# FiLM layer on one core: slab 0 loaded by two DMAs and stored in five parts, the other slabs stored whole

## The chip, the cores and the metric

The kernel runs on one core of a Trainium2 chip. The metric is the device time of one execution in microseconds (us). Four runs of the kernel before the change took 84.0, 84.25, 84.34 and 84.47 us; their median is 84.29 us.

## What is computed

The reference scales and shifts every row of `x` by a gamma and a beta that belong to its batch entry:

```
batch, seq, dim, cond_dim = 32, 512, 256, 64      # all float32
gamma = conditioning @ gamma_proj                 # [32, 256]
beta  = conditioning @ beta_proj                  # [32, 256]
out   = x * (1 + gamma[:, None, :]) + beta[:, None, :]
```

`x` and `out` hold 16.78 MB each. All other inputs together hold 0.14 MB.

## The kernel before

`x` is cut into four slabs of eight batch entries (`SLABS`). A slab is one tile `xs0` to `xs3` of 128 partitions by 32 rows by 256 elements (4 MB). Each partition holds 32 rows that follow each other in HBM, so a partition's share of a slab is one run of 32 KB. Sixteen partitions belong to one batch entry, so each partition needs one gamma row and one beta row for the whole slab. All four slabs stay in on-chip memory and are changed in place; no buffer is used twice.

**Loads.** The SyncE queue (SP in the profile) issues all loads of `x` in L60. `LOADS` cuts slab 0 into four DMAs of 8 rows, that is 128 runs of 8 KB each. Slabs 1, 2 and 3 come in one DMA each, 128 runs of 32 KB. The ScalarE queue (ACTq) issues the three small loads, `conditioning` (L49), `gamma_proj` (L51) and `beta_proj` (L52).

**Gamma and beta.** TensorE spreads the transposed conditioning over 512 columns (L73), VectorE copies it out of PSUM (L75), and one matmul for each slab (L80) gives a PSUM tile `gb_p` with the gamma row and the beta row of every partition. ScalarE copies it into `gb_s`, adding 1 to gamma (L83, L86), because GpSimd (POOL) reads `gb_s`, while VectorE (DVE) reads `gb_p`.

**Arithmetic.** Each slab is worked in two groups of 16 rows (`GROUP`). VectorE takes the first 11 rows of a group (`ON_DVE`) with two instructions, L101 (add 1, multiply) and L104 (add beta). GpSimd takes the other 5 rows with L103 (multiply) and L105 (add). In the built program GpSimd does both multiplies of a slab before both adds.

**Stores.** The ScalarE queue issues the stores in L111, behind its own copies. `STORES` gives the rows at which a slab's stores end. Slabs 0 and 3 are stored as two halves of 16 rows (runs of 16 KB), each when its group is done. Slabs 1 and 2 are stored whole (runs of 32 KB) after their second group.

**Semaphores of the DMAs.** The framework gives DMAs completion semaphores from a set of eight and reuses them. A DMA that gets a used one waits on its issuing queue until the earlier DMA of that semaphore has landed. In the kernel before, the load of slab 2 waits in this way for the first load of slab 0, and the load of slab 3 for `beta_proj`.

Of the kernel before, what the change touches and what calls it, by code (L numbers as in the profile page):

```python
# [2 lines left out]

# [5 lines left out]


@with_exitstack
def kernel(
    ctx: ExitStack,
    tc: tile.TileContext,
    x: bass.AP,
    conditioning: bass.AP,
    gamma_proj: bass.AP,
    beta_proj: bass.AP,
    out: bass.AP,  # L20
):
    nc = tc.nc
    f32 = mybir.dt.float32
    ALU = mybir.AluOpType

    batch, seq, dim = x.shape
    cond_dim = conditioning.shape[1]
    P = 128
    SLABS = 4
    BS = batch // SLABS  # L30
    REP = P // BS
    ROWS = BS * seq // P
    assert SLABS * BS == batch and REP * BS == P and ROWS * REP == seq

    x_v = x.flatten_outer_dims().rearrange("(s p r) d -> s p r d", s=SLABS, p=P)
    o_v = out.flatten_outer_dims().rearrange("(s p r) d -> s p r d", s=SLABS, p=P)

    LOADS = {0: [8, 8, 8, 8]}
    STORES = {0: (16, 32), 1: (32,), 2: (32,), 3: (16, 32)}
    GROUP = 16  # L40
    ON_DVE = 11

    consts = ctx.enter_context(tc.tile_pool(name="consts", bufs=1))
    xpool = ctx.enter_context(tc.tile_pool(name="xpool", bufs=1))
    psum = ctx.enter_context(tc.tile_pool(name="psum", bufs=1, space=bass.MemoryType.PSUM))


    cond_s = consts.tile([batch, cond_dim], f32)
    nc.scalar.dma_start(out=cond_s, in_=conditioning)  # L49
    gbproj = consts.tile([cond_dim, 2 * dim], f32)  # L50
    nc.scalar.dma_start(out=gbproj[:, :dim], in_=gamma_proj)  # L51
    nc.scalar.dma_start(out=gbproj[:, dim:], in_=beta_proj)  # L52

    slabs = []
    for s in range(SLABS):
        xs = xpool.tile([P, ROWS, dim], f32, name=f"xs{s}")
        slabs.append(xs)
        r = 0
        for n in LOADS.get(s, [ROWS]):
            nc.sync.dma_start(out=xs[:, r : r + n, :], in_=x_v[s, :, r : r + n, :])  # L60
            r += n
        assert r == ROWS


    ident = consts.tile([batch, batch], f32)
    make_identity(nc, ident)
    rident = consts.tile([batch, batch * REP], f32)
    nc.vector.tensor_copy(  # L68
        out=rident.rearrange("p (b g) -> p b g", g=REP),
        in_=ident.to_broadcast([batch, batch, REP]),  # L70
    )
    cond_T_p = psum.tile([cond_dim, batch * REP], f32)
    nc.tensor.matmul(cond_T_p, lhsT=cond_s, rhs=rident, start=True, stop=True)  # L73
    cond_T = consts.tile([cond_dim, batch * REP], f32)
    nc.vector.tensor_copy(out=cond_T, in_=cond_T_p)  # L75

    gb_p, gb_s = [], []
    for s in range(SLABS):
        p_t = psum.tile([P, 2 * dim], f32, name=f"gb_p{s}")
        nc.tensor.matmul(p_t, lhsT=cond_T[:, s * P : (s + 1) * P], rhs=gbproj,  # L80
                         start=True, stop=True)
        s_t = consts.tile([P, 2 * dim], f32, name=f"gb_s{s}")
        nc.scalar.activation(out=s_t[:, :dim], in_=p_t[:, :dim],  # L83
                             func=mybir.ActivationFunctionType.Identity,
                             bias=1.0, scale=1.0)
        nc.scalar.copy(out=s_t[:, dim:], in_=p_t[:, dim:])  # L86
        gb_p.append(p_t)
        gb_s.append(s_t)

    def rows(t, n):  # L90
        return bass.AP(tensor=t.tensor, offset=t.offset, ap=[t.ap[0], [0, n], t.ap[1]])

    for s in range(SLABS):
        xs = slabs[s]
        g_p, b_p = gb_p[s][:, :dim], gb_p[s][:, dim:]
        g_s, b_s = gb_s[s][:, :dim], gb_s[s][:, dim:]
        for r0 in range(0, ROWS, GROUP):
            v = xs[:, r0 : r0 + ON_DVE, :]
            w = xs[:, r0 + ON_DVE : r0 + GROUP, :]
            nv, nw = ON_DVE, GROUP - ON_DVE  # L100
            nc.vector.scalar_tensor_tensor(out=v, in0=rows(g_p, nv), scalar=1.0, in1=v,  # L101
                                           op0=ALU.add, op1=ALU.mult)
            nc.gpsimd.tensor_tensor(out=w, in0=w, in1=rows(g_s, nw), op=ALU.mult)  # L103
            nc.vector.tensor_add(out=v, in0=v, in1=rows(b_p, nv))  # L104
            nc.gpsimd.tensor_tensor(out=w, in0=w, in1=rows(b_s, nw), op=ALU.add)  # L105
            done = r0 + GROUP
            if done in STORES[s]:
                e0 = 0
                for e1 in STORES[s]:
                    if r0 < e1 <= done or STORES[s] == (ROWS,):  # L110
                        nc.scalar.dma_start(out=o_v[s, :, e0:e1, :], in_=xs[:, e0:e1, :])  # L111
                    e0 = e1


# [1 line left out]
_INS = ['x', 'conditioning', 'gamma_proj', 'beta_proj']  # L116
_OUTS = [((32, 512, 256), 'float32')]


# [23 lines left out]
```

## Time and profile before

| | |
|---|---|
| median of 4 runs | 84.29 us (84.0 to 84.47) |
| the profiled execution | 84.94 us, of which its span is 83.2 us |
| DVE busy | 50.1 us in 18 instructions |
| POOL busy | 46.3 us in 22 instructions |
| PE, ACT busy | 9.1 us, 3.9 us |
| moved by DMA | 33.69 MB, 405 GB/s over the span |

The profiled execution has 1.74 us around its span, and it is 0.65 us above the median of the runs. Times inside the profile count from the start of the span. q1 is the DMA queue of the SyncE engine (the loads of `x`), q10 that of the ScalarE engine (the small loads and all stores). A core has 16 DMA engines, and both queues run on all of them. A DMA over 128 partitions gives each engine 8 packets, one for each contiguous run, and ends with a completion packet of 4 bytes. Besides the views, the trace holds one record for every DMA packet, with queue, size, start and duration, and the time at which each of a DMA's sixteen engines reported completion. Where a text speaks of packet records or completion records, it means these.

### The profile page before, as it was taken

The page shows a single profiled execution, that of the slowest core. Times are in us where ns is not written, and L with a number is a line of the kernel's source. Part 1 is how long each engine was busy: PE and PEld are TensorE (multiplying, and loading weights), DVE is VectorE, ACT ScalarE, POOL GpSimd, SP SyncE. Part 2 cuts the span into 40 slices and gives each one's busy share as a digit, 9 for nine tenths or more (in the row PEclk, how much of TensorE's full clock was granted, in tenths as well). Part 3 has the DMA queues.
Part 4 walks back from the last instruction along what each step waited for, and adds up shares of the span by engine and source line. Part 5 has one row for each costly group of instructions (what it writes and reads, how often), then busy time and mean ns, then how long its engine had stood idle before and what let it go on. Part 6 is the DMA issues. An engine that isn't in the chain of part 4 may idle for free.

```text
span 83.2 us, 155 instructions
## 1 busy us (share of the span) xinstructions
PE 9.1 (11%) x10; PEld 2.8 (3%) x10; DVE 50.1 (60%) x18; ACT 3.9 (5%) x9; POOL 46.3 (56%) x22
## 2 busy tenths in 40 slices
PE   0080499900000000000000000000000000000000
PEld 0010243100000000000000000000000000000000
DVE  1003019999999999965999994399999500000000
ACT  0600033330000000000000000000000000000000
POOL 2000029999999999805999990399999100000000
DMA  2899999969979999997999999699899969899980
GB/s 51 319 435 379 428 422 540 473 299 504 489 339 426 402 536 441 378 457 307 433 449 465 520 394 465 292 504 489 378 394 504 473 299 489 370 441 441 394 378 8
DMA packets 2080, 33.69 MB, mean 405 GB/s; under 512 B 288, under 2 KB 416, under 8 KB 416
## 3 DMA queue, kind: packets, MB, share of 16 engines
q1 hardware_dynamic: 1008, 16.78, 48.1%
q10 hardware_dynamic: 1072, 16.92, 47.5%
HBM read 16.92 MB, written 16.78 MB: 405 GB/s over the span
## 4 chain that ended last, share of the span: by engine, by line
DMA 62%; DVE 15%; ACTq 1%; issue 0%; DVEq 0%
DMA xs<-in_x_dram 53%; DMA gbproj<-in_beta_proj_dram 9%; DVE xs L104 7%; DVE xs L101 7%; ACTq L51 1%; ACTq L49 0%; DVEq L101 0%
## 5 line engine op out<-in xcount | busy, mean ns | idle before, releaser
L103 POOL TENSOR_TENSOR xs<-xs,gb_s 128x1280 f32<-128x1280 f32 x8 | 23.0, 2894 | 17.9 <-ACT gb_s L83 10.9
L101 DVE SCALAR_TENSOR_TENSOR xs<-gb_p,xs 128x2816 f32<-128x2816 f32 x8 | 24.7, 3087 | 9.4 <-ACT gb_s L86 5.1
L104 DVE TENSOR_TENSOR xs<-xs,gb_p 128x2816 f32<-128x2816 f32 x8 | 24.7, 3087 | 0.3
L105 POOL TENSOR_TENSOR xs<-xs,gb_s 128x1280 f32<-128x1280 f32 x8 | 23.0, 2888 | 0.0
L80 PE MATMUL gb_p<-gbproj,cond_T 64*128 64x512 f32 x8 | 7.2, 1074 | 3.1 <-DMA gbproj<-in_beta_proj_dram 3.1
L75 DVE COPY cond_T<-cond_T_p 64x512 f32<-64x512 f32 x1 | 0.7, 683 | 4.8 <-PE cond_T_p L73 4.8
L80 PEld LDWEIGHTS gb_p<-gbproj,cond_T 64*128 64x128 f32 x8 | 2.5, 327 | 7.9 <-issue 7.9
L73 PE MATMUL cond_T_p<-rident,cond_s 32*64 32x512 f32 x2 | 1.9, 1068 | 4.4 <-DMA cond_s<-in_conditioning_dram 4.4
L83 ACT ACTIVATE gb_s<-gb_p 128x256 f32<-128x256 f32 x4 | 1.5, 384 | 11.1 <-PE gb_p L80 11.1
L86 ACT COPY gb_s<-gb_p 128x256 f32<-128x256 f32 x4 | 1.5, 367 | 0.0
L83 ACT ACT_TABLE_LOAD x1 | 1.3, 1283 | 2.4 <-issue 2.4
L68 DVE COPY rident<-ident 32x512 f32<-32x512 f32 x1 | 0.4, 414 | 1.2 <-POOL ident masks.py:199 1.2
L73 PEld LDWEIGHTS cond_T_p<-rident,cond_s 32*64 32x64 f32 x2 | 0.3, 198 | 4.4 <-issue 4.4
masks.py:197 POOL MEMSET ident<- 32x32 f32 x1 | 0.1, 114 | 0.3 <-POOLq L127 0.3
masks.py:199 POOL TENSOR_SCALAR_AFFINE_SELECT ident<-ident 32x32 f32<-32x32 f32 x1 | 0.2, 203 | 0.1
L127 POOL MEMSET const-float32-0.0<- 128x1 f32 x1 | 0.1, 103 | 0.2 <-issue 0.2
L127 POOL MEMSET const-bfloat16-1.0<- 128x1 bf16 x1 | 0.1, 106 | 0.0
L127 POOL MEMSET const-uint8-127<- 128x1 uint8 x1 | 0.1, 106 | 0.0
L127 POOL MEMSET const-float32-1.0<- 128x1 f32 x1 | 0.1, 103 | 0.0
## 6 DMA issues: line engine op xcount, KB each, us to landing
xs<-in_x_dram SPq DMA_DIRECT2D x3, 4096.0 KB, 32.5
out_dram<-xs ACTq DMA_DIRECT2D x4, 2048.0 KB, 17.6
out_dram<-xs ACTq DMA_DIRECT2D x2, 4096.0 KB, 23.9
xs<-in_x_dram SPq DMA_DIRECT2D x4, 1024.0 KB, 8.8
gbproj<-in_gamma_proj_dram ACTq DMA_DIRECT2D x1, 64.0 KB, 6.6
gbproj<-in_beta_proj_dram ACTq DMA_DIRECT2D x1, 64.0 KB, 7.6
cond_s<-in_conditioning_dram ACTq DMA_DIRECT2D x1, 8.0 KB, 3.5
```

Source lines behind the costliest of these rows:

```text
L51: nc.scalar.dma_start(out=gbproj[:, :dim], in_=gamma_proj)
L68: nc.vector.tensor_copy(out=rident.rearrange("p (b g) -> p b g", g=REP), in_=ident.to_broadcast([batch, batch, REP]),)
L73: nc.tensor.matmul(cond_T_p, lhsT=cond_s, rhs=rident, start=True, stop=True)
L75: nc.vector.tensor_copy(out=cond_T, in_=cond_T_p)
L80: nc.tensor.matmul(p_t, lhsT=cond_T[:, s * P : (s + 1) * P], rhs=gbproj, start=True, stop=True)
L83: nc.scalar.activation(out=s_t[:, :dim], in_=p_t[:, :dim], func=mybir.ActivationFunctionType.Identity, bias=1.0, scale=1.0)
L86: nc.scalar.copy(out=s_t[:, dim:], in_=p_t[:, dim:])
L101: nc.vector.scalar_tensor_tensor(out=v, in0=rows(g_p, nv), scalar=1.0, in1=v, op0=ALU.add, op1=ALU.mult)
L103: nc.gpsimd.tensor_tensor(out=w, in0=w, in1=rows(g_s, nw), op=ALU.mult)
L104: nc.vector.tensor_add(out=v, in0=v, in1=rows(b_p, nv))
L105: nc.gpsimd.tensor_tensor(out=w, in0=w, in1=rows(b_s, nw), op=ALU.add)
L127: nc = _bacc.Bacc("TRN2", target_bir_lowering=False, num_devices=1)
```

## The change

Slab 0 is loaded by two DMAs, one of 8 rows and one of 24 rows; the second is described as three runs of 8 KB for each partition (`max_dma_last_dim`). Slab 0 is stored by five DMAs of 2, 2, 4, 8 and 16 rows; the first four are issued after the first group's instructions, the last after the second group's. Slab 3 is stored whole, like slabs 1 and 2. There were 3 small loads, 7 loads of `x` and 6 stores; there are 3, 5 and 8.

```diff
-    LOADS = {0: [8, 8, 8, 8]}
-    STORES = {0: (16, 32), 1: (32,), 2: (32,), 3: (16, 32)}
+    LOADS = {0: [8, 24]}
+    RUN = {0: 8}
+    STORES = {0: (2, 4, 8, 16, 32), 1: (32,), 2: (32,), 3: (32,)}
...
-            nc.sync.dma_start(out=xs[:, r : r + n, :], in_=x_v[s, :, r : r + n, :])
+            nc.sync.dma_start(out=xs[:, r : r + n, :], in_=x_v[s, :, r : r + n, :],
+                              max_dma_last_dim=RUN.get(s, ROWS) * dim * 4)
...
-            done = r0 + GROUP
-            if done in STORES[s]:
-                e0 = 0
-                for e1 in STORES[s]:
-                    if r0 < e1 <= done or STORES[s] == (ROWS,):
-                        nc.scalar.dma_start(out=o_v[s, :, e0:e1, :], in_=xs[:, e0:e1, :])
-                    e0 = e1
+
+            for e0, e1 in zip((0,) + STORES[s], STORES[s]):
+                if r0 < e1 <= r0 + GROUP:
+                    nc.scalar.dma_start(out=o_v[s, :, e0:e1, :], in_=xs[:, e0:e1, :])
+        assert STORES[s][-1] == ROWS
```

In the built program the order of the compute instructions on every engine is as before (their lines are 2 higher: L101 is now L103, L104 is L106, and on GpSimd L103 is L105, L105 is L107). The waits differ in three places. The first instruction on each of VectorE and GpSimd now waits for the 24-row load, where it waited for the second 8-row load. The load of slab 2 now waits for `gamma_proj`, and the load of slab 3 for the 24-row load. The stores of slabs 2 and 3 wait, besides their data, for two earlier stores of slab 0.

## Prediction

> **What bounds the kernel now.** I read the page's DMA row first, then the queues, then the chain, to see whether engines or transfers set the end.
>
> ```profile
> span 83.2 us, 155 instructions
> ...
> DMA  2899999969979999997999999699899969899980
> ...
> q1 hardware_dynamic: 1008, 16.78, 48.1%
> q10 hardware_dynamic: 1072, 16.92, 47.5%
> ```
>
> The DMA row gives the mean busy share of the 16 DMA engines in 40 slices of 2.08 us. It is 9 nearly everywhere. The queue lines say the same in sum: 48.1% + 47.5% = 95.6% of 83.2 us, 79.5 us for each engine. The remaining 3.7 us lie at the ends: the packet records begin at 1.77 us, the last completion comes at 82.34 us (0.86 us before the end), and the engines finish at different times (fifteen report the last store between 81.17 and 81.62 us, one at 82.34). The 6s and 7s inside are no gaps: a count of open packets over time finds all sixteen engines busy from 2.0 to 80 us, and the stretches agree (times, then PE, PEld, DVE, ACT, POOL, clock, DMA share, GB/s):
>
> ```profile
> 4.00:12.00 8.00, 4.48 (x5) 1.45 (x6) 0.68 (x1) 0.47 (x2) 0.00 (x1) 1.00 1.02 413
> ...
> 66.00:80.00 14.00, 0.00 (x0) 0.00 (x0) 0.00 (x0) 0.00 (x0) 0.00 (x0) 1.00 1.00 430
> ```
>
> A share over 1 comes from packets counted whole where they start. After 66 us no engine computes, and DMA is still full for 14 us. The chain of waits seems to say otherwise:
>
> ```profile
> 9.33 43.89 DMA xs<-in_x_dram
> ...
> 59.56 3.02 DVE xs L101
> 62.57 0.02 issue
> 62.59 3.09 DVE xs L104
> ```
>
> It goes through slab 3's load (issued at 9.33 us, landed at 53.22) and VectorE, and stops at 65.7 us. But the store that follows it lands 16.6 us after its issue at 65.77 us. Its 2 MB take one engine only 8 x 0.611 = 4.9 us; for the other 11 us or so it stood behind older stores. So the work per DMA engine sets the end, and the chain has room.
>
> Last the stalls of the two computing engines:
>
> ```profile
> POOL xs L103 <- DMA xs<-in_x_dram: 7.0, 3, 3.4
> DVE xs L101 <- ACT gb_s L86: 5.1, 1, 5.1
> DVE xs L101 <- DMA xs<-in_x_dram: 4.2, 2, 2.6
> ```
>
> VectorE lost 4.2 us to loads of slabs 2 and 3. The change can win that back, and it will not reach the end by itself.
>
> **Packet prices.** The packet records have nearly constant durations: 46 ns for 1 KB, 309 for 8 KB, 611 for 16 KB, 1213 for 32 KB, 9 for a completion. That is 9 ns plus 37.6 ns per KB ((1213 - 611)/16). So I estimate 84 ns for 2 KB and 159 for 4 KB, which do not occur here; the neighbours on both sides lie on the line.
>
> **Loads of slab 0.** Before, each engine takes 4 x 8 packets of 8 KB, 32 x 0.309 = 9.89 us. After, 8 + 24 packets of 8 KB, the same; two completions less, -0.02 us. If the three runs of a partition were sent as one of 24 KB, it would be 24 x 0.309 - 8 x 0.911 = 0.13 us less; the built program keeps 3 runs, so I take 0.
>
> **SP's queue.** Five issues instead of seven (327 to 647 ns each) change nothing, since the engines are already fed. Slab 2's load now waits for gamma (landed at 7.8 us; it was issued at 5.85), slab 3's for the 24-row load (about 13.9 us, was 9.33). No other work stands behind them on SP. They are covered by queued loads: slab 0 lasts to about 13, slab 1 to 22.8, slab 2 to 32.5 us. A wait would cost its length beyond those times, so 0.
>
> **The first compute.** VectorE and POOL started at 12.2 and 12.0 us. Now they need all of slab 0; in the completion records its last part is in at 13.85 us. I take 14.0 us, 1.9 us later. Behind the first instructions the whole stream of VectorE and POOL is queued. VectorE does a group in 6.15 us ((36.8 - 12.2)/4), so without stalls its eight groups end at 14.0 + 49.2 = 63.2 us, 2.5 us earlier than now.
>
> **Stores, when they come.** Rows 0 to 8 of slab 0 are VectorE's and ready at 20.2 us. Rows 8 to 16 wait for POOL's third instruction, 14.0 + 3 x 2.87 = 22.6 us; the last 16 rows for 26.4; slabs 1, 2 and 3 for 38.7, 51.0 and 63.3 us. ACT has nothing else to do then, so its order blocks nothing.
>
> **Who gets the engines.** From 24 to 36 us the records show each engine taking one load packet of 32 KB, then one store packet of 16 KB, in turn. With 2 KB stores the loads therefore run almost alone. The first store was issued at 20.63 us and its first packet started at 24.31, so I put the first new one at 20.2 + 3.7 = 23.9. Nine of the 24 large load packets of an engine have started by then; 15 remain, 15 x 1.213 = 18.2 us, with 15 packets of 2 KB between them, 1.3 us. Loads end at about 43.4 us instead of 52. What is left of slab 0's stores, 8.7 us, lasts to 52.1, slab 1's 9.7 us to 61.8, slab 2's to 71.5, slab 3's to 81.2. Each is issued before the one ahead of it ends: 38.7 against 52.1, 51.0 against 61.8, 63.3 against 71.5. Storing slab 3 whole thus gives up its half-way start and loses nothing while 8.2 us (4.5 after a pickup of 3.7) cover it.
>
> **The sum.** Slab 0's stores: 8 x (84 + 84 + 159 + 309 + 611) ns = 9.98 us against 16 x 0.611 = 9.78, +0.20, with three more completions +0.03. Slab 3's store: 8 x 1.213 = 9.70 against 9.78, -0.07, one completion less -0.01. Loads -0.02. Together +0.13 us.
> Two prices remain. The 32 KB load packets were stretched by 0.31 us per engine in sum, 0.29 of it between 24 and 36.5 us beside 16 KB stores (about 7 packets, 41 ns each; the largest 1433 - 1213 = 220 ns), but by only 0.02 us afterwards, beside the same kind of stores. In place of this come 15 load packets beside tiny stores: from nothing (-0.31) to 15 x 41 ns (+0.31); I take 0, the middle, as the rows show both. Small stores might be dearer than the line: the 1 KB reads cost on average 10% over theirs (0.403 against 0.368 us per engine), at worst 72 ns for 46. Ten per cent on the 2 and 4 KB packets (2.6 us) is +0.26; below the line they can't well go, since 37.6 ns per KB holds at every size. I take 0, as most rows lie on the line.
> So the profiled execution goes from 84.94 to 85.07 us, and the median from 84.29 to 84.42.
>
> [...] The row first: the two 64 KB loads of gamma and beta ran between 5.2 and 8.5 us, and the stretch from 4 to 12 us shows no idle DMA engine around them. [...]
>
> **The rivals.** *Slower, by contention.* Each remaining load packet meets a small store, and the turn between reading and writing stretches it. For it: the 0.29 us between 24 and 36 us. Against it: hardly any stretch from 36.5 to 52 us. At twice the old mean, 15 x 82 ns - 0.31 + 0.13 gives +1.05, 85.3 us; at the largest stretch everywhere, +3.1, 87.4. It decides from (0.42 + 0.31 - 0.13)/15 = 40 ns per load packet.
> *Faster, by the chain.* If the chain's end counted, its 2.5 us would show, 81.8 us. Against it: the last store's wait of 11 us. What would remain is smaller: no stretch, joined runs, 84.42 - 0.31 - 0.13 = 83.98, not enough; only if the one late engine (0.7 us behind, already so at the first load's completion, 5.83 against 5.10 us) also came level would it be 83.3.
> *The queue runs dry before slab 3.* Should compute slip by over 4.5 to 8.2 us, each further microsecond counts whole. Nothing in the built order suggests it.
>
> **How the numbers follow.** Half a per cent, 0.42 us, is about what a measurement of this kernel can tell from no change. The forecast, nothing measurable, gets 0.65; contention 0.20 and the dry queue 0.03; the faster cases 0.12. The range runs from 83.9 (no stretch, joined runs, run-to-run spread) to 85.0 (+0.31 and +0.26 on the forecast).
>
> **What would show it.** The DMA row should stay at 9; the queues' shares should add to about 95%. First compute near 14 us, no stall of VectorE on `xs` later, its end near 63 us, loads done near 43, the last store landing near 82. A later last completion with 2 KB or 4 KB packets above the line, or load packets above 1213 ns, means contention; a hole in the DMA row between 60 and 75 us, the dry queue; a gain of over 0.4 us means that I overrate the packets' work as the bound.

## The result, and the profile after

The changed kernel takes 84.70 us (median of 44 runs, 84.46 to 85.99) against 84.44 us (median of 63 runs, 83.87 to 86.53). The ratio is 1.0043, with a 95% interval of 1.0025 to 1.0061: 0.36 us longer (0.21 to 0.52), below the half per cent that was called no change. Ratios, here and below, leave out runs in a slower state that some executions show (the medians are then 84.66 and 84.30 us), so they differ a little from those of the medians of all runs. The time lies inside the range and 0.28 us above the forecast; 0.15 us of that is the base, 84.44 us over 63 runs instead of 84.29 over four. The runs of each kernel spread over more than the effect, and those of the two kernels not in the same way: 32 of the 63 runs before took less than 84.46 us, the lowest time of the changed kernel.

The profiled execution took 84.78 us, with a span of 83.0 us. That is less than before's 84.94 and 83.2, though the runs say the opposite. The completion records show why: in the profile before, one DMA engine was 0.7 us behind the others from the first load on and ended last; in the profile after none was (last store done between 81.48 and 82.16 us). A pair of single profiles can't be compared by their spans at this size; the work inside can. These are the changed kernel's DMA row and queues on the page:

```profile
span 83.0 us, 154 instructions
...
DMA  2899999969979969899699999989998998999890
...
q1 hardware_dynamic: 976, 16.78, 48.6%
q10 hardware_dynamic: 1360, 16.92, 47.7%
```

The DMA engines are as full as before: 96.3% of 83.0 us is 79.97 us per engine by the packet records, against 79.49, so 0.48 us more work. There are 288 packets more on q10, the small stores. The chain, however, looks entirely different (start, length, what):

```profile
1.72 7.67 DMA gbproj<-in_beta_proj_dram
...
13.71 3.09 DVE xs L103
...
59.66 0.02 issue
59.68 3.09 DVE xs L106
```

The loads of slabs 2 and 3 are on it no more. VectorE starts at 13.7 us, from then on works without a stall on `xs`, and ends at 62.8 us instead of 65.7. In the waits, only gamma and beta seem to hold the engines up:

```profile
POOL xs L105 <- ACT gb_s L85: 12.6, 1, 12.6
...
DVE xs L103 <- ACT gb_s L85: 6.9, 1, 6.9
```

The views are wrong about that start. The copy named there ended at 13.70 us and is slab 1's; slab 0's was done at 12.25 us. What both engines waited for is the 24-row load: its last part landed at 13.57 us by the completion records, and the instructions that wait for its semaphore went on at 13.6 us. In the kernel with four rows first (below) the same load landed at 14.08 us and VectorE started at 14.20; there the view names it:

```profile
DVE xs L103 <- DMA xs<-in_x_dram: 7.0, 1, 7.0
```

So the change does what it can for the computing engines behind the start: that comes 1.5 us later, but the 4.2 us of load stalls are gone, and 2.9 us are won at the end of the chain. None of it reaches the end, because the last store, issued at 62.85 us, then waits for the same queue of stores (slab 2's lands at 72.5 us).

### The profile page after: what moved, and what is told of

Same layout as the page of the kernel before. It is cut to its first block, busy times and chain, and to the rows that moved or that the text cites. A ratio compares the mean times of both kernels' runs of the same rounds, so it can differ in the third digit from the quotient of the medians.

```text
span 83.0 us, 154 instructions
## 1 busy us (share of the span) xinstructions
PE 9.1 (11%) x10; PEld 2.8 (3%) x10; DVE 49.9 (60%) x18; ACT 3.9 (5%) x9; POOL 46.2 (56%) x22
## 4 chain that ended last, share of the span: by engine, by line
DVE 49%; issue 11%; DMA 9%; PE 5%; ACTq 1%; ACT 0%
DVE xs L103 29%; DVE xs L106 19%; DMA gbproj<-in_beta_proj_dram 9%; PE gb_p L82 5%; ACTq L52 1%; ACTq L50 0%; ACT gb_s L85 0%
## 5 line engine op out<-in xcount | busy, mean ns | idle before, releaser
L105 POOL TENSOR_TENSOR xs<-xs,gb_s 128x1280 f32<-128x1280 f32 x8 | 23.0, 2894 | 12.6 <-ACT gb_s L85 12.6
L103 DVE SCALAR_TENSOR_TENSOR xs<-gb_p,xs 128x2816 f32<-128x2816 f32 x8 | 24.7, 3084 | 6.9 <-ACT gb_s L85 6.9
L106 DVE TENSOR_TENSOR xs<-xs,gb_p 128x2816 f32<-128x2816 f32 x8 | 24.7, 3087 | 0.3
L107 POOL TENSOR_TENSOR xs<-xs,gb_s 128x1280 f32<-128x1280 f32 x8 | 23.0, 2892 | 0.0
## 6 DMA issues: line engine op xcount, KB each, us to landing
out_dram<-xs ACTq DMA_DIRECT2D x3, 4096.0 KB, 21.9
```

## Where the 0.48 us of work come from

The packet records price it. The new sizes cost exactly what the line through the others gave: all 2 KB packets 84 ns, all 4 KB ones 159 ns. The packets at their prices make 78.64 us against 78.51, the +0.13 of the prediction. The rest is stretch, time that packets took beyond their price: 32 KB load packets were stretched by 0.72 us per engine in sum, against 0.31 before (shorter load packets by 0.05 us less than before). And it lies elsewhere than before. From 24 to 40 us, where every load packet alternated with a 2 KB store, there is none at all; the whole of it is in the last two load packets of each engine, 50 ns on average in the last but one and 664 ns in the last (largest 851). The stretches of the changed kernel (times, PE, PEld, DVE, ACT, POOL, clock, DMA share, GB/s) show it:

```profile
26.00:40.00 14.00, 0.00 (x0) 0.00 (x0) 13.93 (x6) 0.00 (x0) 14.00 (x6) 1.00 1.02 438
41.60:44.00 2.40, 0.00 (x0) 0.00 (x0) 2.40 (x1) 0.00 (x0) 2.40 (x2) 1.00 0.96 288
```

In the second row the engines are about as busy as in the first (0.96 against 1.02), and move 288 instead of 438 GB/s. The busy share doesn't tell here how fast a packet goes.

## The experiments

Theory A: the work of the DMA engines, packet prices plus that stretch, sets the time. Theory B: the stretch was a chance of one execution. Theory C: the loads, or slab 3 stored whole, cost the time.

### One part at a time

**Five stores only.**

```diff
-    STORES = {0: (16, 32), 1: (32,), 2: (32,), 3: (16, 32)}
+    STORES = {0: (2, 4, 8, 16, 32), 1: (32,), 2: (32,), 3: (16, 32)}
```

> The kernel before, with only slab 0's stores cut into 2, 2, 4, 8 and 16 rows (loads and slab 3's stores as before). Theory A (the work of the DMA engines sets the time, and the profile after shows two additions: +0.13 us of packet prices, and +0.4 us because the last load packet of each engine, alone beside small stores, was stretched by 0.66 us): packet prices +0.23, stretch moved to the last load as in the changed kernel, so +0.5 to +0.7 us, about 85.0; loads done near 43 us. Theory B (the stretch in the profile after is a chance of that one execution; only packet prices count): +0.2 us, and no stretch at the last load. Theory C (the time comes from the loads of slab 0 or from slab 3 stored whole): no change.

Measured: 85.20 us against 84.58, ratio 1.0072 (1.0038 to 1.0107), +0.61 us. The last load packet was stretched by 506 ns on average, so the stretch is no chance of one execution. The loads were done at 44.5 us.

```profile
26.00:40.00 14.00, 0.00 (x0) 0.00 (x0) 13.89 (x6) 0.00 (x0) 14.00 (x6) 1.00 1.02 438
41.70:44.00 2.30, 0.00 (x0) 0.00 (x0) 2.30 (x2) 0.00 (x0) 2.30 (x2) 1.00 0.91 294
```

But more is lost than in the whole change, which the theories didn't foresee. The completion records and SyncE's instructions show a third term. At the end SyncE waits for the completion semaphores one after another in a fixed order, about 63 ns each, and only then does the closing sequence run. Before and after the change the last store has the last semaphore in that order, and the span ends 0.83 us after its landing. Here there are 19 DMAs instead of 16, the last store has the first semaphore, and the span ends 1.14 us after it: +0.31 us that have nothing to do with the data. SyncE's closing waits on stores (L138 stands for the closing sequence; us in total, times, longest), in the kernel before:

```profile
SPq L138 <- DMA out_dram<-xs: 72.4, 5, 43.8
```

and with five stores only, where one wait takes it all and the others come behind it:

```profile
SPq L138 <- DMA out_dram<-xs: 68.2, 1, 68.2
```

**Loads only.** `LOADS` and `RUN` as changed, stores as before.

> The kernel before, with only slab 0's loads changed (8 rows, then 24 rows in three runs of 8 KB). A and B: same packets, so within 0.1 us of before; first compute at 13.7 us instead of 12.0, and it doesn't matter. C: a good part of the measured +0.3 us shows here.

Measured: 84.56 against 84.58 us, ratio 1.0013 (0.9978 to 1.0048). The medians are as A and B said, and the later first compute, with the first store at 22.3 us, costs nothing that shows in them. But the interval reaches to +0.41 us, so it doesn't exclude C for the loads, and the spread of the runs speaks for a part of it: none of the twelve took less than 84.47 us (the changed kernel's lowest is 84.46), while 15 of the 35 runs before did. The profile explains some of this: the span ends 0.95 us after the last landing (14 DMAs), 0.12 us more than before, and the load packets beside 16 KB stores were stretched by 0.51 us instead of 0.31. The rest stays open.

**Slab 3 whole only.** `STORES[3]` is `(32,)`, all else as before.

> The kernel before, with only slab 3 stored whole. A and B: -0.08 us by packet prices, so hardly to be told from before; the store is issued at 65.8 us while slab 2's store is still queued until about 71. C (the half-way start was needed): +0.2 us or more.

Measured: 84.51 against 84.58 us, ratio 0.9997 (0.9960 to 1.0034). The store was issued at 65.9 us, and slab 2's landed at 72.8. C gets no support here: the interval ends at +0.29 us, and the lowest time is 83.92 us against 83.91.

**Five stores on slab 3 instead.** `STORES[3]` is `(2, 4, 8, 16, 32)`, slab 0 in halves.

> The kernel before, with slab 3 instead of slab 0 stored in 2, 2, 4, 8 and 16 rows, at a time when no load is left. A: the packet prices alone, +0.23 us (84.65), no new stretch, so 0.3 to 0.4 us faster than the five stores on slab 0. B: +0.2 us, the same as the five stores on slab 0. C: no change.

Measured: 85.10 against 84.58 us, ratio 1.0070 (1.0026 to 1.0114), +0.59 us, the same as with the five parts on slab 0. The stretch is not there (29 ns in the last load packet), and 19 DMAs again end 1.14 us before the span's end: +0.23 for packets and +0.31 for the end waits make +0.54. So by medians the stretch costs little. By the lowest time of each kernel's runs it does cost: 83.91 before, 84.33 with the parts on slab 3, 84.87 with the parts on slab 0. The intervals are too wide to decide.

### More and other small stores, one queue

**Sixteen parts of 2 rows.** `STORES[0]` is `tuple(range(2, 33, 2))` in the changed kernel.

> The changed kernel, with slab 0 stored in sixteen parts of 2 rows. A2: packet prices 16 x 8 x 84 ns = 10.75 us instead of 9.98, +0.77, and 11 completions +0.10; the last load packet again stretched by about 0.6 us, as the packets behind it are small; end waits +0.2: about 1.0 us slower than the changed kernel, 85.7. B: +0.9 plus the end waits, hardly different in time, but the last load packet isn't stretched every time. If small packets cost more than the line of the other sizes, 2 KB records above 84 ns.

Measured: 93.31 against 84.50 us, ratio 1.1043 (1.1004 to 1.1083), far beyond what was expected, by another cause. The page's DMA row has holes:

```profile
DMA  3899999995559999889998999999978990099990
```

On average a DMA engine had nothing to do for 2.2 us between 20 and 28 us and for 4.3 us around 78 us. Who waited (the SyncE queue's own waits: us in total, times, longest):

```profile
SPq L61 <- DMA out_dram<-xs: 41.0, 2, 25.3
```

With 27 DMAs on eight semaphores, the loads of slabs 2 and 3 got semaphores that small stores used just before. They were issued at 27.4 and 43.5 us instead of 7.5 and 13.6. That is a rival I had priced as a dry queue, reached through the semaphores. The packets at their prices make 79.51 us against 78.64, the +0.87 that was expected; the 2 KB packets took 84 ns again (median; 88 on average). The last load packets before the loads ran out, at 39 us, were stretched by 561 ns.

**No 2 KB parts.** `STORES[0]` is `(4, 8, 16, 32)` in the changed kernel.

> The changed kernel, with slab 0 stored in parts of 4, 4, 8 and 16 rows, no 2 KB packets. Packet prices -0.09 us against the changed kernel; end waits +0.06. A2: if the stretch of the last load packet comes from the small packets beside and behind it, it is smaller with 4 and 8 KB (0.2 to 0.4 us), so 0.2 us faster than the changed kernel, 84.5. B: 0.03 us faster, 84.7.

Measured: 85.10 against 84.50 us, ratio 1.0074 (1.0035 to 1.0113). Not faster; the last load packet was stretched by 542 ns, so stores of 4 KB bring it too. Neither theory gives +0.6 us: the packets are +0.05 dearer than before and the end waits +0.06. In the profile two engines ended 0.9 us after the rest; both had started the last load late and had the longest packets.

**All stores behind the loads on one queue.**

```diff
-                    nc.scalar.dma_start(out=o_v[s, :, e0:e1, :], in_=xs[:, e0:e1, :])
+                    nc.sync.dma_start(out=o_v[s, :, e0:e1, :], in_=xs[:, e0:e1, :])
```

> The changed kernel, with all stores issued on the SyncE queue behind the loads instead of on the ScalarE queue, so that every DMA engine finishes its loads before its first store. Theory A2 (time = packet prices + stretch of load packets that meet stores + up to 0.31 us of waits at the end when the last store's semaphore is an early one in the list): the same packet prices as the changed kernel (+0.13 us against before), no load packet above 1213 ns after 13 us, same end: 0.1 us faster than before, 84.3 to 84.4, and 0.4 us faster than the changed kernel. Theory B (packet prices alone, the stretch costs nothing or is hidden): +0.13, 84.6, like the changed kernel. Theory D (an engine that serves loads and stores in turn moves more than one that serves one kind): slower than the changed kernel.

Measured: 85.05 against 84.50 us, ratio 1.0074 (1.0039 to 1.0109). My expectation was wrong: with all loads of `x` and all stores on one queue the kernel is about 0.6 us slower than before. The execution that was profiled took 88.07 us, 3 us more than the median, so its profile can't say where. Theory D would have it so, but this interval and that of the changed kernel (1.0025 to 1.0061) overlap; D is neither shown nor excluded.

**The same, with every slab in one load and one store.**

> All stores on the SyncE queue behind the loads, and every slab loaded by one DMA and stored by one DMA: 64 packets of 32 KB for each engine. A2: loads 38.82 us instead of 39.0, stores 38.82 instead of 38.96, five completions less: -0.37 us; no stretch beside stores, -0.25; but the last store takes an early semaphore, +0.2 us: together -0.4 us, about 84.1. Loads end near 41 us, stores 32 KB each follow without a hole. B: -0.2 us. D: slower than before. Should compute be late for slab 3 (issue near 63 us against 70 us when slab 2's store ends) the DMA row would show a hole.

Measured: 85.05 against 84.50 us, ratio 1.0057 (1.0023 to 1.0091); wrong again, and here the profile says where most of it went. Gamma and beta alternate packet by packet with loads of 32 KB instead of 8 KB. The chain:

```profile
1.71 17.32 DMA gbproj<-in_beta_proj_dram
...
21.92 3.10 DVE xs L103
```

Beta landed at 19.0 us instead of 9.3 and VectorE started at 21.9 us. Slab 3's store was issued at 71.07 us, when slab 2's was done, and the engines idled 0.6 us. Its load packets of `x` were also stretched by 1.25 us per engine, where those of the kernel before were by 0.95 (8 and 32 KB). Both kernels keep the runs of 8 KB in slab 0; beside those beta landed at 9.3 us before and 9.4 us after the change.

### Four kernels with half stores

To keep the number of DMAs at 16, or to shift the last semaphore, these issue some stores as two DMAs of 64 partitions:

```diff
-                    nc.scalar.dma_start(out=o_v[s, :, e0:e1, :], in_=xs[:, e0:e1, :])
+                    halves = 2 if s in HALVED else 1
+                    for h in range(halves):
+                        q = slice(h * P // halves, (h + 1) * P // halves)
+                        nc.scalar.dma_start(out=o_v[s, q, e0:e1, :], in_=xs[q, e0:e1, :])
```

**End waits (`HALVED = {0, 1}` in the kernel before).**

> The kernel before, with the stores of slabs 0 and 1 each issued as two DMAs of 64 partitions: the same packets, three DMAs more, so that the last store gets the first semaphore in the list at the end instead of the last. Theory E (the last store's place in that list costs about 63 ns for each wait behind it, as the profiles of the five-store kernels show): +0.31 us and +0.03 for three completions, so about 0.34 us slower than before, and 1.14 us from the last landing to the end of the span instead of 0.83. Rival (those waits are hidden, or only the profiled execution has them): +0.03 us.

**Two halves (`{1, 2, 3}`).**

> The changed kernel, with slab 0 stored in two halves as before; the stores of slabs 1, 2 and 3 are each issued as two DMAs of 64 partitions, so that there are 16 DMAs and the end waits stay as in the changed kernel. Theory A2 (the five stores cost their packets, 0.22 us, and about 0.4 us for the stretched last load packet): 0.1 us faster than before, 0.3 to 0.4 us faster than the changed kernel, no stretch at the last load. Rival B (the stretch costs nothing in the end): 0.2 us faster than the changed kernel.

**Large packets (all slabs).**

> A version meant to beat both: slab 0 loaded as 8 rows and then 24 rows in runs of 24 KB, all slabs stored whole, each store as two DMAs of 64 partitions (16 DMAs, the last store on the last semaphore). Packet prices: -0.13 us for the loads, -0.08 for each of slabs 0 and 3, so -0.28 against before; gamma and beta come later, as each of their packets waits for one of 24 KB (about 12 us instead of 9.3), which a slack of several us covers. If prices decide: 84.15, ratio 0.997. If the engines need the loads to end early (near 43 us), or a store comes late, a hole in the DMA row and a slower kernel.

**Eight rows first (`{1, 2}`).**

> The changed kernel, with slab 0 stored in parts of 8, 8 and 16 rows (slabs 1 and 2 each as two DMAs of 64 partitions, 16 DMAs in all). Packet prices -0.14 us against the changed kernel. If the stretch of the last load packet needs small packets beside or behind it, it is well below the 0.5 to 0.66 us that stores of 2 and 4 KB gave; if it comes from the loads ending early, whatever the store's size, it is as large.

Measured against 84.69 us: end waits 96.78 us, ratio 1.141; two halves 109.16, 1.287; large packets 109.19, 1.292; eight rows first 104.62, 1.229. All intervals are within 0.01 of these. I had taken the halves as free: the same bytes in the same packets, all in flight together. The page of the two-halves kernel shows what they do (GB/s in 40 slices of 2.7 us):

```profile
DMA  3999999999898999998999899899899999999520
GB/s 79 404 393 407 495 399 459 483 399 423 356 489 375 405 477 441 399 471 375 441 193 193 230 230 193 230 242 242 217 278 193 217 338 205 217 350 230 145 97 12
```

From 53 us on only half stores are left, the engines are busy, and the rate is little over half: 243 GB/s from 52 to 80 us against 424 from 26 to 52. A 32 KB packet of a half store took 2.49 us (median) instead of 1.21, and each half store ran on sixteen engines (sixteen completion packets). Why such a packet takes twice as long no run here shows.

So the times of these four answer nothing about their questions, and whether a version beats both kernels stays open. Two readings come from before the halves begin, or from beside them. With end waits, the span ends 1.14 us after the last landing, as expected (19 DMAs). With eight rows first, where no store under 8 KB exists and the halves begin only at 53 us, the last load packet of every engine took 1213 ns: no stretch. With the 16 KB stores of the kernel before it was stretched by 17 ns on average. So in the four kernels that had stores of 2 or 4 KB queued when the loads ran out the last load packet was stretched by 506 ns or more on average, and in the other profiles that are read here by 29 ns at most (with large packets the last but one was, by 418 ns, beside half stores). That the loads end early is not enough for it, as far as one profile shows: with eight rows first they ended at 49.3 us, between the 44.5 of the changed kernel and the 53.2 of before. Why it comes stays open.

## Why the prediction was right, and what was off in it

The direction and the verdict held, for the reason given: the time is the DMA engines' work, and the compute chain has room. It was close all the same: 0.36 us is near the 0.42 us at which a change was to count, and the sum, +0.13 us, lies below the measured interval. Step by step:

- **Saturation and cover.** Right. The DMA row stayed near 9; compute started at 13.7 us (forecast 14.0); VectorE ended at 62.8 (63.2), loads at 44.5 (43.4); the stores were issued at 38.35, 50.60 and 62.85 us (38.7, 51.0, 63.3). No store came late.
- **Packet prices.** Right to the nanosecond: 84 and 159, and +0.13 us in sum.
- **Slab 3 whole, loads in two DMAs.** By the medians both are too small to see, as forecast (0.9997 and 1.0013), but the intervals are as wide as the whole effect, and the lowest times leave the part of the loads open.
- **Stretch.** This term was mis-sized. I took 0 net and put the contention on fifteen load packets beside small stores, up to 41 ns each. Measured: 0 on them, and 0.51 to 0.66 us on the last one; net +0.40 us in the profile. With it the sum is +0.53, without it +0.13; the runs gave +0.36 (0.21 to 0.52), so the packet prices alone are too little and the whole stretch of one profile a little too much. The 0.31 us that I set against it is one profile's, too. In the four kernels with 16 KB stores and no halves the sum was 0.22, 0.23, 0.31 and 0.51 us (mean 0.32); in the three with stores of 2 or 4 KB that kept the queues full it was 0.52, 0.55 and 0.72 (mean 0.60). With the 0.28 us between the means the sum is +0.41, inside the interval. This is arithmetic on single profiles: no run takes the stretch alone away, and the loads' part stands beside it as a rival. The contention rival expected stretch and put it in the wrong place; that the turn between reading and writing causes it was my guess, and no run shows it. The largest stretch before, too, was 321 ns (a packet of 1534 ns at 34.9 us), not the 220 ns that its upper figure rests on.
- **The end.** I took the 0.86 us behind the last completion as fixed. It is fixed for these two kernels only because both have 16 DMAs. Any experiment that changes the count moves it by up to 0.31 us; with that, the five stores alone (0.23 + 0.31, and the stretch) and the whole change (0.13, and the stretch) no longer contradict each other.
- **The late engine.** I priced it as part of a faster case; it came and went between executions: one engine ended 0.7 us late in the profile before and 0.9 us late with slab 3 whole, none did after the change or with loads only.

## What to carry to other kernels

Where the DMA engines are busy from end to end, as here (95.6% of the span before, 96.3% after), sum the packets at their own durations. The 4.2 us of load stalls that the change removed didn't shorten the kernel, and five parts of a store instead of two cost 0.23 us in packets, of 0.59 and 0.61 us measured; 0.31 us of those lay at the end. So look at both ends: what a small early transfer alternates with (beta landed at 9.3 us beside packets of 8 KB, at 19.0 us beside 32 KB), and on which semaphore the last store lands (0.83 us from landing to the end of the span with the last semaphore, 1.14 us with the first). Cut DMAs by rows rather than by partitions (2.49 us instead of 1.21 for a packet of a half store), and count them: with sixteen parts, reused semaphores made two loads wait 41.0 us in all for stores.

## What the runs showed of the hardware that I had not expected

- A 32 KB packet of a store over 64 partitions took 2.49 us (median); in a store over 128 it took 1.21 us.
- The closing waits cost about 63 ns for each semaphore behind the last store's: 0.83 us from landing to the end of the span in the best order, 0.89 and 0.95 with slab 3 whole and loads only, 1.14 in the worst.
- The last load packet, with 2 or 4 KB stores queued, took 1.7 to 1.9 us on average instead of 1.21; with 8 or 16 KB stores it took 1.21 to 1.24 us.
- Loads alone were not at full rate in one profile: in the eight-rows-first kernel the 32 KB packets took 1359 ns until the first store came, and 1213 ns from then on (393 and 426 GB/s in these stretches):

```profile
12.00:24.00 12.00, 5.11 (x6) 1.46 (x5) 9.59 (x4) 2.59 (x8) 9.64 (x4) 1.00 1.02 393
24.00:36.00 12.00, 0.00 (x0) 0.00 (x0) 11.93 (x5) 0.00 (x0) 12.00 (x5) 1.00 0.99 426
```
